# Moving the sample sequences' state updates from the mixing stage of a hybrid decoder layer into its second feed-forward block

## The chip, the cores and the metric

One core of a Trainium2 chip runs the whole program. The metric is the device time of one execution in microseconds, the median of several runs. The engines are TensorE (PE; PEld is its loading of weights), VectorE (DVE), ScalarE (ACT), GpSimd (POOL) and SyncE (SP, which here only issues DMAs).

## The reference

Two layers of a decoder work on 256 prompt tokens and on 8 sample sequences of 4 tokens each, 288 columns in all. The sample sequences bring carried states and return new ones:

```python
for l in range(DEPTH):
    x = layer_norm(ALPHA * x + 0.5 * swiglu(x, ffn1_w_in[l], ffn1_w_out[l]), ...)
    z = x @ mix_w_in[l]                       # split into RWKV-7, HGRN2 and chunk-gMLP heads
    ...
    mix = concat([o_rw, o_hg, o_cm]) @ mix_w_out[l]
    x = layer_norm(ALPHA * x + mix, ...)
    x = layer_norm(ALPHA * x + 0.5 * swiglu(x, ffn2_w_in[l], ffn2_w_out[l]), ...)

# RWKV-7, each token (state S is value by key, 4 heads of 64 x 64 for each sequence)
S = S * w_t + sa (kk_t a_t)^T + v_t k_t^T ;  o_t = S r_t
# HGRN2 (state is 128 x 128, 4 heads for each sequence)
S = exp(total) * S + sum_s k_s exp(total - cum_s) v_s^T
```

The outputs of the sample tokens need the old states and the four tokens' own rows. The new states are outputs of the program and are read by nothing else in it.

## The kernel before

Activations lie with features on the 128 rows and the 288 tokens as columns. Every dense product is made of 128x128 weight blocks; for precision, weights and operands are split into a high and a low part, and three products are summed (`block`). A block of weights of 512x256 is loaded by SP into `raw` (three buffers), rounded by ACT into `wh`, and its rest is made by DVE, in places by POOL, into `wl` (`prep`, three buffers each).

A layer has three stages: a feed-forward block (`ffn`), the mixing stage (`mix`) and a second feed-forward block. A feed-forward block runs over 11 steps j of 256 columns. Each has a gate and an up product of 48 matmuls each; DVE and ACT scale, shift and multiply them (`zfix`). Then the output product and a layer norm follow (`post`). `ffn` takes a table `mid` of functions that are called ahead of a step; in the second block of a layer and in layer 1's first, step 2 gets the `residual`, eight chunks of two DVE operations and one ACT operation.

The mixing stage interleaves chains, which are Python generators, with the dense products of the input projection as a background (`go`, `CHAINS`, `ORDER`): `prompt`, `pre` and `post` for RWKV-7, `scan` and `hmix` for HGRN2's prompt tokens, `sample` (`rw_sample`) and `hsam` (`hg_sample`) for the sample tokens, `cm` for the gMLP, and the `hou`/`posts` chains that write the operand tiles of the output product. Two chains make the new states:

- `rst` (`rw_states`, line 1255) starts when `sample` is done. `rw_sample` has already made, on POOL, the operands `ub`: the corrections `uv` spread over the 8 sequences. For each of two head pairs PE makes `pns` (a product with `ex`), DVE adds it to the state tile `st`, and POOL multiplies `st` by the decay read from `eP`. Then PE transposes `st` (`pno`), ACT copies it to `no`, and SP issues eight stores.
- `hst` (`hg_states`, line 1541) starts when `hsam` is done. For each of four heads the value rows are spread over the sequences into `hvb`, on ACT for heads 0 and 2 (8 scalings each) and on POOL for heads 1 and 3; POOL multiplies the loaded state `hs` by the decay in `hgP`; PE makes two products `hn`; DVE adds each to half of `hs`; SP issues one store of 512 KB.

The list scheduler of the framework orders each engine's instructions when the program is built: by the order in which they are traced, the lead that `PR` gives a part, and its model of when operands and tile buffers are ready. On the chip each engine then follows that fixed order and waits where an operand is late. Tiles of a tag share a number of buffers (`B`: 19 large `m4` tiles, 11 of `a2`).

The program prints `act`, `mul`, `add` and the like as one helper line each (L62, L65, L77 in the profile), so operations are told apart by their tiles.

Of the kernel before, what the change touches and what calls it, by code (L numbers as in the profile page):

```python
# [2 lines left out]

# [35 lines left out]
class Trunk:  # L39
# [80 lines left out]
    def consts(self):  # L120
# [34 lines left out]
        # causal masks over [s, t]: t > s and t >= s  # L155
# [5 lines left out]
        # block-merge masks: ml[b][t, s] and mt[b][s, t]  # L161
# [13 lines left out]
        # the same for blocks of 64 tokens, in rows of (block parity, token)  # L175
# [19 lines left out]
        # sample block masks over [(h,s), (h,t)], blocks of four tokens  # L195
# [9 lines left out]
        # the same with the rows of head h at the place of head (h + 2) % 4  # L205
# [3 lines left out]
        # row -> batch within a 32-token group, and row -> parity of its head  # L209
# [10 lines left out]
        # sums over a head's 64 rows into 32 equal rows, and their spreading back  # L220
# [11 lines left out]
        # a token's row in each group of 32; minus one at odd rows  # L232
# [3 lines left out]
        # two heads' inclusive sample blocks in either half of the rows  # L236
# [17 lines left out]
        # a token's row in each group of 32, for either pair of heads  # L254
# [3 lines left out]
        # the first four rows repeated for each batch  # L258
# [3 lines left out]
        # token -> batch, and a token's row in each group of 32  # L262
# [4 lines left out]
        # reset points of the running sums: token 0 of each chunk  # L267
# [70 lines left out]
    def prep(self, spec):  # L338
        """A block of weights, loaded and split into high and low parts."""
# [34 lines left out]
    def block(self, spec, x, res, first, last):  # L374
        """A block's share of a product."""
# [26 lines left out]
    def dense_by(self, w, n0s, x, groups):  # L402
        """Several products, each group of chunks through all of them before the next."""
# [7 lines left out]
    def fill(self, n=1):  # L411
        """Goes on with the products in the background by n steps."""
# [18 lines left out]
    def hilo(self, r, name, n=NT):  # L431
        """Rows of high and low parts in turn, of equal rows."""
# [5 lines left out]
    def newx(self, nt):  # L438
        """Operand tiles of a product's moving side: eight 128-row chunks, high and low parts."""
# [9 lines left out]
    def zfix(self, ps, st, nm):  # L449
        """A product's two column blocks, and their biases, with the norm's scale (and shift) applied."""  # L450
# [45 lines left out]
    def post(self, wout, x, nk, coef, ln, shift, groups=None):  # L496
        """Residual sum with a product, and its layer norm: the operand tiles of the next product hold
        (u - m) g in high and low parts, with m the mean of the first six chunks (shift) or of all."""
# [100 lines left out]
    def final(self, po, m6, coef, g, square, i):  # L599
        """The last norm, in rows of tokens, and the outputs; the last rows are the prompt's end and the samples."""  # L600
# [6 lines left out]
        def rows(j, c):  # L607
            """A chunk, times the norm's gain, in rows of tokens."""
# [40 lines left out]
        # the mean's rest as rows of high, low and high parts  # L649
# [34 lines left out]
    def final_load(self, l):  # L684
        """The last norm's shift in each row, and its gain in (negated) rows of high, high and low parts."""
# [10 lines left out]
    def residual_g(self, pend):  # L696
        """The norm's output itself, times ALPHA for the next residual sum."""
# [9 lines left out]
    def residual_x(self):  # L707
        """The same, and operand tiles of it."""
# [11 lines left out]
    def load_x(self, specs):  # L720
        """The operand tiles of the inputs; both loads in halves of the features, and the first weights between."""
# [66 lines left out]
    def rw_pre(self, l, q, zs):  # L788
# [3 lines left out]
        # lora products  # L792
# [3 lines left out]
        else:  # L796
            # tanh(x) = 2 sigmoid(2 x) - 1
# [19 lines left out]
        # running sums of the log decay (in units of -exp(-0.5)), centred in each chunk  # L817
# [17 lines left out]
        # keys  # L835
# [30 lines left out]
        # (sum r k r_k) v, and the norm's shift  # L866
# [13 lines left out]
    def gnorm(self, l, x, n):  # L880
        """Rows of tokens, less the means of n groups of 64, and one over each group's deviation."""
# [12 lines left out]
    def rw_gate(self, q, OT, p, G, BO, m, ts):  # L894
        """The norm's gain and shift, the bonus and the gate, into chunks 0 and 1 of the operand tiles m."""
# [33 lines left out]
    def rw_prompt(self, l, KR, bh, kh, V, eP, em):  # L929
        """Four chunks of 64 tokens; rows are (chunk parity, token), matrices [rows, chunk pair, head, token]."""  # L930
# [8 lines left out]
        # token-major values, first keys beside AT[1] in the order of its matrices, second keys  # L939
# [15 lines left out]
        def heads(j=None, i=None):  # L955
            """Chunk pair, parity, head pair, head, its rows, its columns and its matrix."""
# [7 lines left out]
        def pairs(name, f):  # L964
            """Products of both head parities, in turn in the array's two row halves."""
# [9 lines left out]
        for qi, src in ((0, bh), (2, kh)):  # L975
# [13 lines left out]
            if qi == 0:  # L989
                # the inverse over pairs of tokens, and its transpose  # L990
# [12 lines left out]
        # token-major values, keys and (negated) first operands  # L1003
# [15 lines left out]
        # inverses over twice as many tokens, from I - (the block between two halves) times the inverse  # L1019
# [25 lines left out]
        # corrections without the state, and their dependence on it  # L1045
# [11 lines left out]
        # from one chunk's state to the next, and to the outputs  # L1057
# [3 lines left out]
        # decay from a chunk's centre to its end, and on to the next chunk's centre  # L1061
# [36 lines left out]
        # token-major outputs  # L1098
# [31 lines left out]
    def rw_load(self, l):  # L1130
        nc, I = self.nc, self.I
        # carried states, rows (parity of the batch, value)
# [7 lines left out]
    def rw_sample(self, l, KR, bh, kh, V, eP):  # L1140
# [9 lines left out]
        # the carried states transposed to rows (head, key)  # L1150
# [8 lines left out]
        # keys and queries of each batch alone  # L1159
# [4 lines left out]
        # A matrices: rows (h, s), or (h + 2, s) for those that meet values  # L1164
# [19 lines left out]
        # [row, head pair, head, token]: rows A_rb and A_rk of each pair  # L1184
# [11 lines left out]
        # token-major values (rows swapped by two heads) and keys  # L1196
# [8 lines left out]
        # rows of each pair block-expanded by head  # L1205
# [18 lines left out]
        # solve for the corrections  # L1224
# [6 lines left out]
        # the queries' products  # L1231
# [16 lines left out]
        ub = [v512(self.a2(f"ub{l}{c}")) for c in range(2)]  # L1248
        for c in range(2):
            self.mul(ub[c].rearrange("p (b v) -> p b v", b=8), uv[:, c].unsqueeze(1).to_broadcast([128, 8, 64]),  # L1250
                     self.mb.unsqueeze(2).to_broadcast([128, 8, 64]), gp)
        yield
        self.rws = ST, exv, ub, eP

    def rw_states(self, l):
        """The sample states after their tokens."""
        nc, O = self.nc, self.O
        gp = nc.gpsimd
        SS = slice(T, NT)
        ST, exv, ub, eP = self.rws  # L1260
        no = self.m4([128, 2, 4, 2, 64], f"no{l}")
        for c in range(2):
            p = self.ps(f"pns{l}{c}")
            self.mm(p, exv[:, c].rearrange("p h n -> p (h n)"), ub[c])
# [276 lines left out]
    def hg_states(self, l):  # L1541
# [5 lines left out]
        for h in range(4):  # L1547
# [10 lines left out]
            if h in E["hs"]:  # L1558
                self.mul(s0, s0, tot.to_broadcast([128, 8, 128]), gp)
# [273 lines left out]
```

## Time and profile before

| | us |
|---|---|
| runs of the kernel | 1373.8, 1374.07, 1381.42 |
| median | 1374.07 |
| span of the profiled execution | 1379.8 |
| PE busy | 1308.3 (95%) |
| DVE busy | 1009.8 (73%) |
| ACT busy | 663.8 (48%) |
| POOL busy | 274.1 (20%) |

The span is the time from the first to the last instruction of the one execution that was profiled. The stages of layer 0 lie at about 10 to 240 us (first feed-forward block), 240 to 485 us (mixing, with its output product and norm) and 485 to 690 us (second feed-forward block); layer 1 repeats them up to 920, 1155 and 1375 us. In the rows below, an instruction row of a timeline has start, duration, engine, source line, operation, output and inputs, shapes and count; a bracket at its end is the idle time before it and what ended it. Neighbouring instructions of one kind are merged into one row with a count.

### The profile page before, as it was taken

The page shows a single profiled execution, that of the slowest core. Times are in us where ns is not written, and L with a number is a line of the kernel's source. Part 1 is how long each engine was busy: PE and PEld are TensorE (multiplying, and loading weights), DVE is VectorE, ACT ScalarE, POOL GpSimd, SP SyncE. Part 2 cuts the span into 40 slices and gives each one's busy share as a digit, 9 for nine tenths or more (in the row PEclk, how much of TensorE's full clock was granted, in tenths as well). Part 3 has the DMA queues.
Part 4 walks back from the last instruction along what each step waited for, and adds up shares of the span by engine and source line. Part 5 has one row for each costly group of instructions (what it writes and reads, how often), then busy time and mean ns, then how long its engine had stood idle before and what let it go on. Part 6 is the DMA issues. An engine that isn't in the chain of part 4 may idle for free.

```text
span 1379.8 us, 27635 instructions
## 1 busy us (share of the span) xinstructions
PE 1308.3 (95%) x11161; PEld 1255.1 (91%) x11162; DVE 1009.8 (73%) x1844; ACT 663.8 (48%) x1052; POOL 274.1 (20%) x381
## 2 busy tenths in 40 slices
PE   7999999898987999999999999998889889999998
PEld 6999999877876999999999999997778789999997
DVE  3555448977877998774698775599986889977643
ACT  4454435762345554443465443368333645544433
POOL 9200001435554100000100000033464421000002
PEclk9999999987997999999999999999999889999999
DMA  5655554531123655554455555554212544555551
GB/s 175 187 168 168 162 165 150 154 106 34 48 86 113 187 156 158 165 168 153 155 168 167 167 156 161 167 160 131 78 31 71 149 124 145 168 161 161 175 168 58
DMA packets 208158, 194.12 MB, mean 141 GB/s; under 512 B 15911, under 2 KB 206363, under 8 KB 208030
## 3 DMA queue, kind: packets, MB, share of 16 engines
q1 hardware_dynamic: 207326, 190.91, 44.9%
q0 software_dynamic: 608, 1.31, 0.4%
q8 instruction: 88, 1.44, 0.4%
q14 instruction: 40, 0.33, 0.1%
q10 hardware_dynamic: 96, 0.13, 0.1%
HBM read 185.10 MB, written 7.22 MB: 139 GB/s over the span
## 4 chain that ended last, share of the span: by engine, by line
PE 79%; DVE 14%; issue 3%; ACT 2%; POOL 1%; DMA 0%; POOLq 0%; SPq 0%; DVEq 0%; ACTq 0%
PE d L97 71%; DVE wl L65 2%; DVE hgO L77 1%; ACT wh L62 1%; DVE yrw L77 1%; DVE hgQ L77 1%; PE pA L97 1%; DVE hR L65 1%; DVE hAT L94 1%; PE hO L97 0%; PE hA L97 0%; DVE ax L65 0%; PE pD L97 0%; POOL hgP L65 0%; DVE hL L65 0%
## 5 line engine op out<-in xcount | busy, mean ns | idle before, releaser
L97 PE MATMUL d<-x,wh 128*128 128x290 f32 (+1 forms) x3968 | 824.0, 301 | 2.5 <-DVE x L77 2.5
L97 PEld LDWEIGHTS d<-x,wh 128*128 128x128 f32 x3968 | 653.3, 192 | 9.8 <-DVE x L77 4.3
L97 PE MATMUL d<-x,wl 128*128 128x290 f32 (+1 forms) x1984 | 602.5, 304 | 16.2 <-ACT x L62 12.4
L62 ACT ACTIVATE wh<-raw 128x1024 fp32r<-128x1024 f32 x344 | 357.2, 1039 | 456.1 <-PE d L97 312.1
L65 DVE TENSOR_TENSOR wl<-raw,wh 128x1024 fp32r<-128x1024 f32 x324 | 395.1, 1220 | 239.4 <-ACT wh L62 238.1
L97 PEld LDWEIGHTS d<-x,wl 128*128 128x128 f32 x1984 | 380.5, 192 | 21.5 <-ACT x L62 15.5
L97 PE MATMUL d<-h,wh 128*128 128x288 f32 x1408 | 282.0, 296 | 0.0
L97 PEld LDWEIGHTS d<-h,wh 128*128 128x128 f32 x1408 | 226.2, 188 | 0.2
L97 PE MATMUL d<-h,wl 128*128 128x288 f32 x704 | 207.8, 295 | 0.0
L65 POOL TENSOR_TENSOR lnv<-lnq,lnq 128x288 f32<-128x288 f32 x6 | 8.2, 1375 | 848.7 <-ACT lnq L62 848.7
L97 PEld LDWEIGHTS d<-h,wl 128*128 128x128 f32 x704 | 132.5, 188 | 0.2
L65 POOL TENSOR_TENSOR wl<-raw,wh 128x1024 fp32r<-128x1024 f32 x20 | 50.0, 2502 | 66.3 <-ACT wh L62 66.3
L62 ACT ACTIVATE h<-sg 128x288 fp32r<-128x288 f32 x88 | 38.1, 435 | 24.5 <-DVE sg L65 20.9
L62 ACT ACTIVATE sg<-yg,ccg 128x288 f32<-128x288 f32 x66 | 34.3, 528 | 29.9 <-DVE yg L77 29.9
L62 ACT ACT_TABLE_LOAD x37 | 47.5, 1283 | 1.4 <-PEq L1821 0.8
L65 DVE TENSOR_TENSOR h<-sg,h 128x288 fp32r<-128x288 f32 x88 | 39.6, 452 | 5.6 <-ACT h L62 5.6
L77 DVE SCALAR_TENSOR_TENSOR ax<-d,ax 128x288 f32<-128x288 f32 x48 | 21.4, 452 | 29.4 <-PE d L97 29.4
L77 DVE SCALAR_TENSOR_TENSOR yu<-nu,ccu,yu 128x288 f32<-128x288 f32 x66 | 33.9, 514 | 0.8
L77 DVE SCALAR_TENSOR_TENSOR yg<-nu,ccg,yg 128x288 f32<-128x288 f32 x66 | 33.8, 515 | 0.8
L62 ACT ACTIVATE lnq<-ax 128x288 f32<-128x288 f32 x48 | 20.9, 435 | 26.2 <-DVE ax L77 26.0
L77 DVE SCALAR_TENSOR_TENSOR sg<-yu,ccu,sg 128x288 f32<-128x288 f32 x66 | 33.3, 509 | 0.0
L65 DVE TENSOR_TENSOR yu<-d,rho 128x288 f32<-128x288 f32 x66 | 29.5, 448 | 0.0
(499 smaller groups left out, 1355.2 us busy)
## 6 DMA issues: line engine op xcount, KB each, us to landing
raw<-in_ffn_w_in SPq DMA_DIRECT2D x176, 512.0 KB
raw<-in_ffn_w_out SPq DMA_DIRECT2D x80, 512.0 KB
raw<-in_mix_w_in SPq DMA_DIRECT2D x56, 512.0 KB
raw<-in_mix_w_out SPq DMA_DIRECT2D x12, 512.0 KB
raw<-in_ffn_w_out SPq DMA_DIRECT2D x16, 256.0 KB
hs<-in_state_hgrn SPq DMA_DIRECT2D x8, 512.0 KB
out_hgrn_state_sample<-hs SPq DMA_DIRECT2D x8, 512.0 KB
raw<-in_mix_w_out SPq DMA_DIRECT2D x8, 256.0 KB
```

The costliest lines, as they stand in the source:

```text
L62: self.nc.scalar.activation(out, in_, func, **kw)
L65: (eng or self.nc.vector).tensor_tensor(out, a, b, op=op)
L77: self.nc.vector.scalar_tensor_tensor(out, a, s, b, op0=op0, op1=op1)
L94: self.nc.vector.copy_predicated(out, mask.bitcast(I16), data)
L97: self.nc.tensor.matmul(out, lhsT, rhs, start=start, stop=stop)
```

## The change

The chains `rst` and `hst` leave the mixing stage. Their steps, now one generator of 12 steps, are called in the second feed-forward block of the same layer: two steps each ahead of the column steps 1, 3, 4, 5, 6 and 7. So step 1 has the RWKV state sums, step 3 their transposes and stores, and steps 4 to 7 one HGRN2 head each. `ub` is made there too, on POOL. The decays are copied by ACT into small tiles (`dc`, `tot`) at the end of the sample chains, since `eP` and `hgP` do not live that long. In `hg_states` the variants go: all spreading is done on ACT, and instead of a multiplication on POOL and an addition on DVE, DVE does both in one scalar_tensor_tensor for each sequence and head.

```diff
 # rw_sample
-        ub = [v512(self.a2(f"ub{l}{c}")) for c in range(2)]
-        for c in range(2):
-            self.mul(ub[c]..., uv[:, c]..., self.mb..., gp)
-        yield
-        self.rws = ST, exv, ub, eP
+        dc = self.ep.tile([128, 2, 8], F32, tag="rdc", name=f"rdc{l}", bufs=1)
+        self.act(dc, eP[:, :, SS].rearrange("p c (b t) -> p c b t", t=4)[:, :, :, 3])
+        yield
+        self.rws = ST, exv, uv, dc
...
 # rw_states
         for c in range(2):
+            ub = self.a2(f"ub{l}{c}").rearrange("p c n -> p (c n)")[:, 0:512]
+            self.mul(ub.rearrange("p (b v) -> p b v", b=8), uv[:, c].unsqueeze(1).to_broadcast([128, 8, 64]),
+                     self.mb.unsqueeze(2).to_broadcast([128, 8, 64]), gp)
             p = self.ps(f"pns{l}{c}")
-            self.mm(p, exv[:, c].rearrange("p h n -> p (h n)"), ub[c])
+            self.mm(p, exv[:, c].rearrange("p h n -> p (h n)"), ub)
             stc = ST[:, c]
             self.add(stc, stc, p.rearrange("p (b v) -> p b v", b=8))
-            dc = eP[:, c, SS].rearrange("p (b t) -> p b t", t=4)[:, :, 3:4].to_broadcast([128, 8, 64])
-            self.mul(stc, stc, dc, gp)
+            self.mul(stc, stc, dc[:, c].unsqueeze(2).to_broadcast([128, 8, 64]), gp)
             yield
...
 # hg_sample
-        yield
-        self.hst = S0, k3
+        tot = self.ep.tile([128, 4, 8], F32, tag="htot", name=f"htot{l}", bufs=1)
+        self.act(tot, self.hsm(P).rearrange("p h (b t) -> p h b t", t=4)[:, :, :, 3])
+        yield
+        self.hst = S0, k3, tot
...
 # hg_states
-            if h in E["vb"]:
-                for b in range(8):
-                    self.act(vb[:, b], v, scale=self.mb[0:96, b:b + 1])
-            else:
-                self.mul(vb, v.unsqueeze(1).to_broadcast([96, 8, 128]),
-                         self.mb[0:96].unsqueeze(2).to_broadcast([96, 8, 128]), gp)
-            tot = self.hsm(P)[:, h].rearrange("p (b t) -> p b t", t=4)[:, :, 3:4]
-            if h in E["hs"]:
-                self.mul(s0, s0, tot.to_broadcast([128, 8, 128]), gp)
+            for b in range(8):
+                self.act(vb[:, b], v, scale=self.mb[0:96, b:b + 1])
             yield
             for i in range(2):
                 p = self.ps(f"hn{l}{h}{i}")
-                bs = slice(4 * i, 4 * i + 4)
-                self.mm(p, k3[0:96, 0, h], vb[:, bs].rearrange("p b v -> p (b v)"))
-                if h in E["hs"]:
-                    self.add(s0[:, bs], s0[:, bs], p.rearrange("p (b v) -> p b v", b=4))
-                else:
-                    for b in range(4):
-                        bb = 4 * i + b
-                        self.stt(s0[:, bb], s0[:, bb], tot[:, bb], p[:, 128 * b:128 * b + 128], ALU.mult, ALU.add)
+                self.mm(p, k3[0:96, 0, h], vb[:, 4 * i:4 * i + 4].rearrange("p b v -> p (b v)"))
+                for b in range(4):
+                    bb = 4 * i + b
+                    self.stt(s0[:, bb], s0[:, bb], tot[:, h, bb:bb + 1], p[:, 128 * b:128 * b + 128], ALU.mult, ALU.add)
...
 # run
-            r = self.ffn(l, "ffn2_w_in", "ffn2_w_out", x, st, lambda: q[l]["ln"][2], {2: self.residual}, SHIFT[2])
+            states = chain(self.rw_states(l), self.hg_states(l))
+            mid = {j: lambda: (next(states), next(states)) for j in STATES} | {2: self.residual}
+            r = self.ffn(l, "ffn2_w_in", "ffn2_w_out", x, st, lambda: q[l]["ln"][2], mid, SHIFT[2])
...
 # mix
-            "hst": (lambda: self.hg_states(l), "hsam"),
-            "rst": (lambda: self.rw_states(l), "sample"),
...
-CHAINS = [('prompt', 1), ('pre', 3), ('rst', 1), ('hsam', 1), ('posts', 1), ('hst', 1), ('hmix', 1), ('sample', 1),
+CHAINS = [('prompt', 1), ('pre', 3), ('hsam', 1), ('posts', 1), ('hmix', 1), ('sample', 1),
...
+STATES = (1, 3, 4, 5, 6, 7)
```

In `PR` the entry `'hst.6': 100` goes, in `E` the entries `'vb'` and `'hs'`. Everything else in the diff is comments.

## Rows read from the trace of the kernel before

**Rows 1.** The page: busy time, share of the span and instructions of each engine.

```profile
PE 1308.3 (95%) x11161; PEld 1255.1 (91%) x11162; DVE 1009.8 (73%) x1844; ACT 663.8 (48%) x1052; POOL 274.1 (20%) x381
```

**Rows 2.** Waits of PE, 240 to 485 us: us in total, times, longest.

```profile
PE d L97 <- ACT x L62: 6.2, 1, 6.2
...
PE cO L97 <- DVE cM L65: 5.7, 1, 5.7
...
PE pb L97 <- DVE rn L77: 2.6, 1, 2.6
...
PE d L97 <- DVE ax L77: 0.6, 1, 0.6
```

**Rows 3.** Timeline, 425 to 450 us: start, us, engine, line, operation, count, idle before.

```profile
428.06 1.20 DVE L77 SCALAR_TENSOR_TENSOR hgO<-yo,cco,qs 128x256 f32<-128x256 f32 x4
...
431.69 6.23 DVE L77 SCALAR_TENSOR_TENSOR hgO<-yo,cco,qs 128x256 f32<-128x256 f32 x4
...
432.04 7.99 POOL L65 TENSOR_TENSOR hs<-hs,hgP 128x1024 f32<-128x1024 f32 x4 [8.89 <-PE hp L97]
...
433.64 0.26 ACT L62 ACTIVATE hsqs<-hp 128x128 f32<-128x128 f32 x1
...
437.84 2.46 DVE L65 TENSOR_TENSOR OT<-OT,G 128x256 f32<-128x256 f32 x2
...
438.28 0.42 ACT L62 ACTIVATE x<-OT 128x256 fp32r<-128x256 f32 x1 [4.38 <-DVE OT L65]
...
438.75 0.61 PE L97 MATMUL d<-x,wl 128*128 128x288 f32 x1 [6.20 <-ACT x L62]
...
442.34 0.40 DVE L65 TENSOR_TENSOR x<-OT,x 128x256 fp32r<-128x256 f32 x1
```

**Rows 4.** Timeline, 1098 to 1116 us: the same place in layer 1.

```profile
1108.13 0.61 PE L97 MATMUL d<-x,wl 128*128 128x288 f32 x1 [6.18 <-ACT x L62]
```

**Rows 5.** Windows after both waits: PE, PEld, DVE, ACT, POOL busy; granted clock, DMA.

```profile
438.70:447.30 8.60, 7.62 (x33) 7.28 (x34) 5.53 (x10) 3.00 (x10) 5.25 (x4) 0.51 0.00 0
...
1108.10:1116.80 8.70, 7.75 (x35) 7.40 (x36) 5.62 (x11) 3.09 (x10) 5.23 (x3) 0.53 0.00 1
```

**Rows 6.** Windows of steps 1, 2, 3 and 7, second feed-forward block of layer 0.

```profile
498.80:511.50 12.70, 12.70 (x97) 12.70 (x96) 12.37 (x27) 7.66 (x12) 0.00 (x0) 1.00 0.54 166
...
511.50:524.30 12.80, 12.75 (x95) 12.54 (x94) 12.72 (x29) 8.02 (x12) 0.00 (x0) 1.00 0.53 165
...
524.30:537.10 12.80, 12.80 (x98) 12.80 (x97) 10.82 (x23) 6.14 (x9) 0.00 (x0) 1.00 0.50 161
...
575.40:588.20 12.80, 12.80 (x98) 12.80 (x97) 9.96 (x21) 5.84 (x8) 0.00 (x0) 1.00 0.54 164
```

**Rows 7.** Tiles: count, ns least/median/most, first and last start, forms.

```profile
L65 POOL TENSOR_TENSOR ub<-uv,mb x4: 1041/1132/1255, 334.7 to 1002.0; 128x512 f32<-128x512 f32 x4
...
L65 DVE TENSOR_TENSOR st<-st,pns x4: 671/676/686, 342.3 to 1018.3; 128x512 f32<-128x512 f32 x4
...
L65 POOL TENSOR_TENSOR st<-st,eP x4: 1057/1062/1069, 345.1 to 1019.1; 128x512 f32<-128x512 f32 x4
...
L62 ACT ACTIVATE hvb<-hk,mb x32: 385/387/390, 447.4 to 1123.5; 96x128 fp32r<-96x128 f32 x32
...
L77 DVE SCALAR_TENSOR_TENSOR hSP<-hSP,hgP,hS x8: 339/342/347, 451.3 to 1121.1; 128x128 f32<-128x128 f32 x8
```

**Rows 8.** Timelines of SP's queue and of ACT: store issues, a weight load, its use.

```profile
355.74 7.32 SPq L1278 DMA_DIRECT2D out_rwkv_state_sample<-no  x8
...
537.39 0.37 SPq L347 DMA_DIRECT2D raw<-in_ffn_w_in  x1
...
544.69 1.06 ACT L62 ACTIVATE wh<-raw 128x1024 fp32r<-128x1024 f32 x1 [2.14 <-PE d L97]
```

**Rows 9.** Windows of 4 us after the wait for rn in layers 0 and 1.

```profile
302.00:306.00 4.00, 4.00 (x21) 2.28 (x20) 3.33 (x7) 1.07 (x2) 0.00 (x0) 0.50 0.00 0
...
976.00:980.00 4.00, 2.45 (x20) 1.68 (x20) 4.00 (x11) 0.85 (x2) 0.78 (x1) 1.00 0.00 0
```

More of the change, by code (lines that the diff above doesn't have):

```diff
@@ L2 @@
 from contextlib import ExitStack, contextmanager
+from itertools import chain
 import concourse.bass as bass
@@ L1247, in rw_sample @@
         self.act(self.rwos, pq)
-        ub = [v512(self.a2(f"ub{l}{c}")) for c in range(2)]
-        for c in range(2):
-            self.mul(ub[c].rearrange("p (b v) -> p b v", b=8), uv[:, c].unsqueeze(1).to_broadcast([128, 8, 64]),
-                     self.mb.unsqueeze(2).to_broadcast([128, 8, 64]), gp)
+        dc = self.ep.tile([128, 2, 8], F32, tag="rdc", name=f"rdc{l}", bufs=1)
+        self.act(dc, eP[:, :, SS].rearrange("p c (b t) -> p c b t", t=4)[:, :, :, 3])
         yield
-        self.rws = ST, exv, ub, eP
+        self.rws = ST, exv, uv, dc
     def rw_states(self, l):
@@ L1258, in rw_states @@
         gp = nc.gpsimd
-        SS = slice(T, NT)
-        ST, exv, ub, eP = self.rws
+        ST, exv, uv, dc = self.rws
         no = self.m4([128, 2, 4, 2, 64], f"no{l}")
         for c in range(2):
+            ub = self.a2(f"ub{l}{c}").rearrange("p c n -> p (c n)")[:, 0:512]
+            self.mul(ub.rearrange("p (b v) -> p b v", b=8), uv[:, c].unsqueeze(1).to_broadcast([128, 8, 64]),
+                     self.mb.unsqueeze(2).to_broadcast([128, 8, 64]), gp)
             p = self.ps(f"pns{l}{c}")
-            self.mm(p, exv[:, c].rearrange("p h n -> p (h n)"), ub[c])
+            self.mm(p, exv[:, c].rearrange("p h n -> p (h n)"), ub)
             stc = ST[:, c]
             self.add(stc, stc, p.rearrange("p (b v) -> p b v", b=8))
-            dc = eP[:, c, SS].rearrange("p (b t) -> p b t", t=4)[:, :, 3:4].to_broadcast([128, 8, 64])
-            self.mul(stc, stc, dc, gp)
+            self.mul(stc, stc, dc[:, c].unsqueeze(2).to_broadcast([128, 8, 64]), gp)
             yield
@@ L1537, in hg_sample @@
         self.hos = os
+        tot = self.ep.tile([128, 4, 8], F32, tag="htot", name=f"htot{l}", bufs=1)
+        self.act(tot, self.hsm(P).rearrange("p h (b t) -> p h b t", t=4)[:, :, :, 3])
         yield
-        self.hst = S0, k3
+        self.hst = S0, k3, tot
     def hg_states(self, l):
         nc, O = self.nc, self.O
-        gp = nc.gpsimd
-        P = self.hg("P")
-        S0, k3 = self.hst
+        S0, k3, tot = self.hst
         for h in range(4):
@@ L1782 @@
 PR = {'prep': 250, 'posts': 450, 'hou0': -50, 'scan': 400, 'hsam': -150, 'post': -400, 'res': 50, 'scan.4': 20,
-      'cm.1': 200, 'q1.0': -7, 'hmix': 20, 'hst.6': 100, 'sample.0': -20, 'hmix.7': -20, 'posts@1': -400,
+      'cm.1': 200, 'q1.0': -7, 'hmix': 20, 'sample.0': -20, 'hmix.7': -20, 'posts@1': -400,
       'sample.2': 50, 'houts@0': 200, 'prompt.19': -7, 'houts': 50, 'scan@0': 400, 'houts.0': -50, 'prompt.22': 200,
       'o1': 7}
-E = {'gn': 'v', 'gm': 'v', 'LN': 1, 'th': 't', 'xl': 'p', 'R1': 'p', 'mo': 'r', 'om': '', 'vb': (0, 2), 'hs': (0, 1,
-     2, 3), 'Ab': 'p', 'RV': 'v', 'LL': 'v', 'S': 'p', 'P': 'p', 'KS': 'v'}
+E = {'gn': 'v', 'gm': 'v', 'LN': 1, 'th': 't', 'xl': 'p', 'R1': 'p', 'mo': 'r', 'om': '', 'Ab': 'p', 'RV': 'v', 'LL': 'v', 'S': 'p', 'P': 'p', 'KS': 'v'}
 GROUPS = {'s': ((0, 1), (6, 7), (2, 3, 4, 5)), 't': ((6, 7), (0, 1), (2, 3, 4, 5)), 'r': ((0, 1, 6, 7), (2, 3, 4,
```

## The prediction

> **What bounds the kernel now.** I read the busy shares first: PE is busy 95% of the span, no other engine above 73% [rows 1]. So time can only be won where PE waits or runs at a low clock. In the two feed-forward blocks of a layer PE does neither (12.75 to 12.80 us busy in each 12.8 us step, clock 1.00) [rows 6]. What is to be won lies in the mixing stage, some 240 to 485 us in layer 0 and its copy in layer 1. The list of PE's waits for that stretch has one largest item: the output product waits 6.2 us, once, for ACT's operand tile x; after it come 5.7, 2.6 and many below 2 us [rows 2]. Layer 1 waits 6.18 us at the same place [rows 4].
>
> The timeline around that wait tells what is late. Four scalar_tensor_tensor on DVE (hgO) start at 431.69 and take 6.23 us; the same four shapes took 1.20 us at 428.06. In between, at 432.04, POOL starts four products hs*tot of 128x1024, 7.99 us in one row. The first OT products, also on DVE, follow and end only when POOL is through (2.46 us for two); then ACT splits OT at 438.28, and PE starts at 438.75 [rows 3]. All the slow DVE instructions read two operands from SBUF, as POOL does. The windows show a second cost: in the 8.6 us after the wait the granted clock is 0.51 (layer 1: 0.53 over 8.7 us), PE's lower level of 1.2 GHz, and PE is still idle for 8.60 - 7.62 = 0.98 us of it [rows 5].
>
> **The change, part by part.**
>
> *POOL's four hs*tot and two vb products leave the mixing stage (per layer).* Without them hgO takes its 1.20 us and ends at 431.69 + 1.20 = 432.89. The next OT product has the operands of the x split, 0.40 us [rows 3], so 433.3. ACT is then still busy: it ends hsqs at 433.64 + 0.26 = 433.90. PE started 438.75 - 438.28 = 0.47 us after the split did, so now at 434.37: a wait of some 1.8 us is left, and 438.75 - 434.37 = 4.38 us are won.
>
> *The clock.* Does it still fall after 1.8 us? The nearest rows are two equal waits of 2.6 us for rn: after the one of layer 0 the clock is 0.50, after that of layer 1 it is 1.00 [rows 2, 9]. [...] If the clock holds, the 7.62 busy us at 0.51 shrink to 7.62 x 0.51 = 3.9, and the 0.98 us of idleness, which is DVE's lateness handed on, mostly goes: 8.6 - 3.9 - 0.2 = 4.5 us won. If it falls all the same, only the 0.98 us is won. I take 4.5 and keep 1.0 as the other end.
>
> *The additions hs + hn on DVE leave the output product.* PE's wait for ax behind them, 0.6 us [rows 2], goes.
>
> Per layer: 4.38 + 4.5 + 0.6 = 9.5 us with the clock held, 4.38 + 0.98 + 0.6 = 6.0 without. Two layers: 19 or 12.
>
> *PE's moved products* (pns, pno, hn) keep their shapes and number, so what the mixing stage saves the feed-forward block pays: zero. This would be a loss if they had filled PE's waits; they stand on the chain or beside dense products, so I see none. A gain in the middle of the mixing stage from POOL's freed time (two ub of 1.13 and two st of 1.06 us, 4.4 us per layer [rows 7]) lies between 0 and 4.4; the dense products there hide most of it, so I take 0. The two added copies (tot, dc) are small ACT work like hsqs, at most 2 x 0.26 us, at a place where ACT waits anyway.
>
> *What the second feed-forward block gets.* Its cover is DVE's and ACT's free time per step; PE has none. Steps 4 to 7 each get one head: 8 ACT scalings of 0.387 us = 3.1 us [rows 7] beside 5.84 busy us of 12.8 [rows 6], which fits; and 8 DVE scalar_tensor_tensor of 128x128 reading PSUM, a form that hSP shows at 0.342 us [rows 7]: 2.74 us beside 9.96 of 12.80 [rows 6], which leaves 0.1 us. It just fits. Step 1 is worse: two additions st of 0.68 us = 1.35 on DVE, and 4.4 us of POOL work that can hold DVE as it held hgO. DVE has 0.33, 0.08 and 1.98 us free in steps 1 to 3, since the residual's work is there already [rows 6]. So DVE is late by up to 1.35 + 4.4 - 2.4 = 3.3 us and has no room to catch up before step 8. What PE bears of it is shown by the residual: in its step DVE is busy 12.72 of 12.80 us and PE still does its 95 products in 12.75 us. So the price lies between 0 and 3.3 us per layer; I take 1.4, nearer to the end that the residual shows. The Trainium skill speaks against this part: "SBUF — State Buffer", section "Who interferes with whom", says that a DVE instruction with two SBUF inputs and a GpSimd instruction that reads SBUF exclude each other for a whole instruction, while one with a single SBUF input is not held. By it the zfix products that read PSUM pass, the zfix additions and the low parts of the weights are held, and the new scalar_tensor_tensor never are; the block's price would be the upper 3.3 us.
>
> *Queues.* Twelve stores per layer move along SP's queue into the block: eight of the RWKV state (7.32 us of SP time for the eight, waits included) and four of HGRN2's. Behind a store that waits for DVE or ACT stand the weight loads. A load is issued at 537.39 and, with three raw buffers, first read by the fourth scaling, at 544.69 [rows 8]: 7.3 us less the transfer. A delay of a few us is hidden; I price it at zero. POOL has nothing else in this block, so nothing stands behind ub there [rows 6].
>
> *Sum:* 2 x (9.5 - 1.4) = 16 us. The profiled execution has a span of 1379.8 us, 5.7 above the median of the runs (1374.07) and within them (1373.8 to 1381.42); it would come to 1363.8. The same 16 us from the median give **1358 us**.
>
> **The rivals.**
>
> *Half is given back (1366).* The clock falls after 1.8 us too, or DVE's lateness reaches PE: 12 - 2 x 1.4 = 9, or 19 - 2 x 3.3 = 12 with part of the first. For it: the two unequal outcomes at 2.6 us, and 0.1 us of room in steps 4 to 7. Against: PE's undisturbed steps under the residual. About 8 us faster, 1366.
>
> *Nothing is won (1374).* PE would then wait as long for the next late operand in the same place: ACT's table load ends just before hsqs, and hon, hO and the second hot follow one another. Against it: these follow the same late DVE row, and the 0.98 us is all that PE waited for them.
>
> *Slower: PE waits behind the moved products (1391).* PE takes its products in order. In step 1 pns needs ub from POOL, and pno needs st from POOL, which needs DVE, whose order is full; hn needs eight ACT scalings. If such a product stands in PE's order ahead of its operand, the dense products behind it wait. The wait at cO is of this kind: 5.7 us [rows 2], and a fallen clock after it costs up to half of the following 8 us [rows 5], some 9 us together. Two such waits per layer cost 36 us, net 36 - 19 = 17 us slower, 1391. It decides from one such wait per layer on, where the gain is gone. Against it: ub's inputs lie ready long before the block.
>
> *More is won (1346).* POOL's 4.4 us per layer in the middle of the mixing stage do shorten the chain there, and the block pays nothing: 19 + 8.8 = 28 us.
>
> **Chances.** Forecast 0.56 (its own range 1350 to 1364), half given back 0.18, nothing 0.09, slower 0.09, more 0.08. About 1% (13.7 us) is what a measurement of this kernel tells from no change; the line is 1360.3. Four fifths of the forecast's chance, the case of more, and a little of the half lie below it: 0.45 + 0.08 + 0.02 = 0.55 faster. Within 1%: 0.11 + 0.16 + 0.09 = 0.36. Slower: 0.09. The range from 1347 to 1374 leaves out the slower case (0.09), half of "nothing" and half of "more": 0.175.
>
> **What would show it.** Right: PE's first output product waits under 2 us in both layers, hgO takes about 1.2 us there, and the following window's clock is above 0.9. If the wait is short but the clock is still near 0.5, the clock's step fails. In the second feed-forward block each step should stay near 12.8 us plus the moved products; waits of PE for wl, y or x there would show that DVE's room was too small, and waits of pns, pno or hn for POOL, DVE or ACT that the order was wrong. SP rows of the stores that are followed by late weight loads would put the loss on the queue. The prediction is wrong altogether if hgO stays at 6 us with POOL idle: then POOL was not what held DVE.

## The result and the profile after: 1395 us, slower

The changed kernel takes 1395.28 us (median; 1389.42 to 1400.03) beside 1374.26 us for the kernel before on the same chip: a ratio of 1.0133, 95% interval 1.0092 to 1.0173. The forecast was 1358 us. The profiled execution has a span of 1398.3 us beside 1379.8.

The page's totals, against [rows 1]: PE is as busy a share as before, in a longer span; POOL has 12 instructions and 9 us less, DVE and ACT have 88 instructions more between them.

```profile
PE 1318.6 (94%) x11162; PEld 1257.7 (90%) x11162; DVE 1005.7 (72%) x1892; ACT 681.2 (49%) x1092; POOL 265.0 (19%) x369
```

The stages, cut at the start of each norm's pair of `lnva` products on PE (the last stage runs to the end of the span), in us. The columns are the mixing stage and the second feed-forward block of layer 0 and of layer 1; the first feed-forward blocks differ from before's by 1 us or less. The kernels below the first two are the experiments. Each ratio is to runs of the kernel before on the same chip. The stages are those of the one execution that was profiled, which need not be a median one: the spans of before, after, hp_without_hs and only_hgrn_moved are 1379.8, 1398.3, 1384.5 and 1355.2 us.

| kernel | median | ratio to before, 95% | mix 0 | FFN2 0 | mix 1 | FFN2 1 |
|---|---|---|---|---|---|---|
| before | 1374.3 | | 251.6 | 212.0 | 243.9 | 224.8 |
| after | 1395.3 | 1.0133 (1.0092–1.0173) | 257.5 | 216.7 | 246.7 | 230.0 |
| before_no_steps | 1394.8 | 1.0133 (1.0097–1.0170) | 252.9 | 211.7 | 256.7 | 224.3 |
| idle_steps_back | 1364.4 | 0.9894 (0.9842–0.9947) | 238.9 | 215.9 | 230.7 | 230.3 |
| posts_steps_three | 1362.7 | 0.9883 (0.9840–0.9925) | 237.4 | 215.9 | 228.4 | 230.5 |
| only_hst_idle_steps | 1399.0 | 1.0127 (1.0065–1.0189) | 256.9 | 216.7 | 249.2 | 228.1 |
| idle_steps_no_states | 1355.4 | 0.9847 (0.9812–0.9883) | 238.9 | 211.5 | 230.7 | 224.6 |
| no_root | 1389.5 | 1.0099 (1.0065–1.0132) | 254.1 | 216.6 | 240.2 | 230.7 |
| sample_steps_two | 1381.3 | 1.0038 (1.0010–1.0066) | 248.2 | 216.0 | 240.9 | 230.6 |
| hp_without_hs | 1378.4 | 1.0020 (0.9985–1.0054) | 248.0 | 215.9 | 242.5 | 230.6 |
| rwkv_sample_steps_two | 1363.6 | 0.9898 (0.9865–0.9930) | 235.0 | 216.0 | 234.7 | 229.0 |
| before_no_pool | 1376.4 | 1.0006 (0.9982–1.0031) | 242.3 | 212.4 | 246.1 | 224.9 |
| only_hgrn_moved | 1361.6 | 0.9886 (0.9840–0.9932) | 232.5 | 213.5 | 233.9 | 227.5 |
| only_rwkv_moved | 1384.8 | 1.0061 (1.0034–1.0089) | 250.8 | 213.6 | 242.7 | 227.2 |

So after's loss lies in two places: the second feed-forward blocks got longer by 4.7 and 5.2 us, which the move has to pay, and the mixing stages, out of which work was taken, got longer too, by 5.9 and 2.8 us (the two profiles against each other).

The DVE timeline at the place of [rows 3]: the four hgO in question take 1.20 us, where they took 6.23.

```profile
430.76 1.20 DVE L78 SCALAR_TENSOR_TENSOR hgO<-yo,cco,qs 128x256 f32<-128x256 f32 x4
```

PE's waits in layer 0's mixing stage (us in total, times, longest), against [rows 2]: the 6.2 us for x are 1.8 and the 5.7 us at cO are gone, and the largest is a new one, 8.4 us for hos; hT's and hTs's are new as well.

```profile
PE hot L102 <- ACT hos L63: 8.4, 1, 8.4
...
PE hT L102 <- ACT hvs L63: 3.3, 1, 3.3
...
PE d L98 <- ACT x L63: 1.8, 1, 1.8
PE hTs L102 <- DVE cM L66: 1.7, 1, 1.7
```

PE's timeline there: the instructions that waited, and cO. hTs is the first transpose of HGRN2's sample chain, hT are other transposes of HGRN2, cO is the gMLP's product, and hot are the transposes of hon (the prompt tokens' result) and hos (the sample tokens') that open the last chains of HGRN2.

```profile
415.84 1.09 PE L98 MATMUL cO<-cwt,cvn 128*64 128x128 f32 x16
...
419.46 0.33 PE L102 MATMUL hTs<-ident,hgV 128*128 128x128 f32 x1 [1.70 <-DVE cM L66]
...
423.55 1.12 PE L102 MATMUL hT<-ident,hgV 128*128 128x128 f32 x4 [3.27 <-ACT hvs L63]
...
429.19 0.40 PE L98 MATMUL d<-x,wl 128*128 128x288 f32 x1 [1.82 <-ACT x L63]
...
456.50 0.48 PE L102 MATMUL hot<-ident,hos 128*128 128x128 f32 x1 [8.38 <-ACT hos L63]
```

In the kernel before, hTs and the first half of cO came at 406.6 and 408.0, and the transpose of hos came last of the hot, without a wait:

```profile
406.60 0.27 PE L101 MATMUL hTs<-ident,hgV 128*128 128x128 f32 x1
...
408.00 0.66 PE L97 MATMUL cO<-cwt,cvn 128*64 128x128 f32 x8 [0.18 <-POOL cvn L65]
...
450.27 0.27 PE L101 MATMUL hot<-ident,hos 128*128 128x128 f32 x1
```

ACT's timeline shows what hos waited for. ACT alternates between the sigmoids of the background's last product (qs<-yo,cco) and the roots of HGRN2's norm (hrm, hrm0s), and loads its function table four times, 1.28 us each.

```profile
448.16 0.28 ACT L63 ACTIVATE hsqs<-hp 128x128 f32<-128x128 f32 x1 [9.13 <-PE hp L98]
448.45 1.28 ACT L63 ACT_TABLE_LOAD   x1
449.75 0.54 ACT L63 ACTIVATE qs<-yo,cco 128x288 f32<-128x288 f32 x1
450.30 1.28 ACT L63 ACT_TABLE_LOAD   x1
451.60 0.30 ACT L63 ACTIVATE hrm<-hrm,eps 128x4 f32<-128x4 f32 x1
...
452.33 1.28 ACT L63 ACT_TABLE_LOAD   x1
453.63 0.53 ACT L63 ACTIVATE qs<-yo,cco 128x288 f32<-128x288 f32 x1
454.18 1.28 ACT L63 ACT_TABLE_LOAD   x1
455.48 0.29 ACT L63 ACTIVATE hrm0s<-hrm0s,eps 128x1 f32<-128x1 f32 x1
...
456.10 0.35 ACT L63 ACTIVATE hos<-hp,hrm0s 128x128 f32<-128x128 f32 x1
```

The same stands in layer 1 (a wait of 8.38 us at 1133.44). Behind the transpose of hos in PE's order stand those of hon, which DVE had finished at 438.9 (the first half) and 452.8; PE could not take them. The dense products behind those had not all been ready: the first started at 457.78, just after DVE had made an x (457.28, 0.45 us), which stands in DVE's order behind ho, a product that needs hot. In the kernel before, the sigmoids of that product ran at 426.5 and 431.0.

### The profile page after: what moved, and what is told of

Same layout as the page of the kernel before. It is cut to its first block, busy times and chain, and to the rows that moved or that the text cites. A ratio compares the mean times of both kernels' runs of the same rounds, so it can differ in the third digit from the quotient of the medians.

```text
span 1398.3 us, 27677 instructions
## 1 busy us (share of the span) xinstructions
PE 1318.6 (94%) x11162; PEld 1257.7 (90%) x11162; DVE 1005.7 (72%) x1892; ACT 681.2 (49%) x1092; POOL 265.0 (19%) x369
## 5 line engine op out<-in xcount | busy, mean ns | idle before, releaser
L66 POOL TENSOR_TENSOR lnv<-lnq,lnq 128x288 f32<-128x288 f32 x6 | 8.2, 1374 | 837.7 <-ACT lnq L63 837.7
```

Of the source, the lines that this page charges most:

```text
L66: (eng or self.nc.vector).tensor_tensor(out, a, b, op=op)
```

## The experiments

The theory after reading this: the change takes more out of the mixing stage than work. `go` lets the background products go on by one step after each step of a chain (`fill`). With `rst` and `hst` twelve steps left, and twelve background steps with them. The order that the scheduler then builds is another one, and worse. The rival: the order is the same in effect, and moved work itself costs the 21 us.

**Idle steps in the place of `rst`.** Four steps that do nothing, with their background steps; the states stay in the feed-forward block.

```diff
+            "rst": (lambda: iter([None] * 4), "sample"),
...
-CHAINS = [('prompt', 1), ('pre', 3), ('hsam', 1), ...
+CHAINS = [('prompt', 1), ('pre', 3), ('rst', 1), ('hsam', 1), ...
```

> The changed kernel, but with a chain of four empty steps where the RWKV state chain stood in the mixing stage, so that the four background steps of dense products that followed its steps are traced where they were before. Theory A (the loss is the order: without these background steps the products o1 and o0 and the loads of hs come later in the plan, ScalarE alternates between two tables, PE waits 8.4 us for hos per layer): the hos wait and the added table loads (41 to 37) go, hs is loaded before the last output weights, the 6.2 us wait of before does not come back, and the time is near the forecast, 1350 to 1365 us. Theory B (the loss is the states held in large buffers through the mixing stage, or the moved work itself): nothing of that changes, the time stays at 1390 to 1400 us.

Measured: 1364.4 us, 31 us below after and some 1% below before. PE's waiting instructions in its timeline: hTs stands before cO again, the transpose of hos comes last of the hot and waits for nothing, and at the output product's place PE waits 1.14 us, at the first hot, for ACT's x.

```profile
405.37 0.27 PE L102 MATMUL hTs<-ident,hgV 128*128 128x128 f32 x1
...
414.02 1.12 PE L98 MATMUL cO<-cwt,cvn 128*64 128x128 f32 x8 [5.72 <-DVE cM L66]
...
433.74 0.30 PE L102 MATMUL hot<-ident,hon 128*128 128x128 f32 x1 [1.14 <-ACT x L63]
...
440.29 0.27 PE L102 MATMUL hot<-ident,hos 128*128 128x128 f32 x1
```

By the stage table the mixing stages are 18.6 and 16.0 us shorter than after's, 34.6 together; the difference of the two spans is the same 34.6. All of it is order: four empty steps are the only difference. 21.5 us of it are PE's idle time (66.4 against 44.8 us in both mixing stages), and 13.1 us are longer busy time for the same number of matmuls, which was not taken apart. The sums of the two stages, after and then idle steps:

```profile
sum 504.23, PE 437.87 PEld 386.54 DVE 387.57 ACT 250.49 POOL 194.96; mean PE 218.94 PEld 193.27 DVE 193.79 ACT 125.25 POOL 97.48
```

```profile
sum 469.57, PE 424.75 PEld 382.10 DVE 384.65 ACT 244.50 POOL 186.74; mean PE 212.38 PEld 191.05 DVE 192.33 ACT 122.25 POOL 93.37
```

**Before, without the background steps.** The states stay where they were; only the numbers behind two chains change.

```diff
-CHAINS = [('prompt', 1), ('pre', 3), ('rst', 1), ('hsam', 1), ('posts', 1), ('hst', 1), ...
+CHAINS = [('prompt', 1), ('pre', 3), ('rst', 0), ('hsam', 1), ('posts', 1), ('hst', 0), ...
```

> The kernel before, states still made in the mixing stage, but no background step after the steps of the two state chains (1 to 0 for both in the list of chains). Theory A: the tail takes the order of the changed kernel, hs is loaded after the last output weights, a wait for hos appears, and the time rises to 1390 to 1410 us though nothing is moved. Theory B: same buffers and same work as before, so 1370 to 1380 us.

Measured: 1394.8 us, the loss of the change without the change. PE's waits in layer 0 have after's new rows:

```profile
PE hot L101 <- ACT hos L62: 7.7, 1, 7.7
PE d L97 <- ACT x L62: 6.1, 2, 4.1
PE hT L101 <- ACT hvs L62: 3.0, 1, 3.0
```

Which steps, and does the chain matter? Two runs. First, idle steps for `hst` alone:

```diff
+            "hst": (lambda: iter([None] * 8), "hsam"),
...
-CHAINS = [... ('posts', 1), ('hmix', 1), ...
+CHAINS = [... ('posts', 1), ('hst', 1), ('hmix', 1), ...
```

> The changed kernel with an idle chain for hst alone: eight steps that do nothing, each followed by one background step, as hst had them before; rst stays out. hst starts only when hsam is done, late in the mixing stage, where little of the background is left. Theory A, only the four steps of rst set the order: hot<-hos stays ahead of the dense products, PE waits some 8 us for hos in each layer, 1389 to 1400 us. Theory B, the number of lost steps counts and eight given back are more than enough: 1362 to 1372 us.

Measured: 1399.0 us. Eight steps late in the stage give nothing back. Second, no idle chain, but three background steps instead of one behind each step of `posts`, which starts where `rst` did:

```diff
-CHAINS = [... ('posts', 1), ...
+CHAINS = [... ('posts', 3), ...
```

> The changed kernel with one number different: each step of the chain posts, which like rst starts when sample is done, is followed by three background steps instead of one; there are no idle steps. The loads of hs then stand ahead of four loads of mix_w_out as in the kernel with idle steps, hot<-hos stands last of the three hot products, and there are 37 table loads instead of 41. Theory A, what was lost with rst is only the progress of the background products at that place, whoever gives it: 1360 to 1368 us, as with the idle steps. Theory B, the place of rst itself counts: 1375 to 1395 us.

Measured: 1362.7 us. What counts is how far the background is when `sample` is done, not who drives it.

**What in the bad order costs.** Four runs of the changed kernel, with a number, a function or an operand changed. The root of the HGRN2 norm without its table:

```diff
-        self.act(r, r, AF.Sqrt, bias=self.eps[:, 2:3], scale=1.0 / 128)
+        self.act(r, r, AF.Square, scale=1.0 / 128)
```

> The changed kernel, in which the root of the HGRN2 norm (hrm, hrm0s) is made by ACT as a square, without the added eps; the values that come out of the HGRN2 norm are then others than the reference's. PE's order is the changed kernel's own, hot<-hos stands first as there; what goes is ACT's table loads between the sigmoids and the roots, four of 1.28 us in the last 10 us ahead of hos. Theory A, the table loads are the larger part of the wait for hos: it falls from 8.4 to about 3.3 us in layer 0, and the time by twice that and some clock, to 1379 to 1387 us. Theory B, hos is late for its operands and not for the tables: the wait stays at 7 to 8 us, the time at 1391 to 1397.

Measured: 1389.5 us. PE's order in the mixing stages stayed, matmul for matmul. The wait for hos fell from 8.4 to 4.5 us, but the time by 5.8 us only, less than expected: the tables are half of that wait and about a fifth of the 31 us.

```profile
452.21 0.47 PE L102 MATMUL hot<-ident,hos 128*128 128x128 f32 x1 [4.46 <-ACT hos L63]
```

The Trainium skill, "ScalarE: Activation LUTs", section "Table sets: the hidden batching unit", asks that all calls of one set be made before those of the next. The trace agrees: the sigmoids and roots that alternate paid four loads of 1.28 us, those of the order with idle steps one between them.

Next, two background steps behind each step of `hsam`, which brings the transpose of hos to the last place of the hot and the sigmoids ahead of the roots:

```diff
-CHAINS = [... ('hsam', 1), ...
+CHAINS = [... ('hsam', 2), ...
```

> The changed kernel with one number different: each step of the chain hsam is followed by two background steps instead of one. Nothing is moved or left out. In the order as built this brings the product hot<-hos to the last place of the three hot products and puts ACT's two sigmoids ahead of the roots, but the loads of hs still stand as late in SP's queue as in the changed kernel (behind eight loads of mix_w_out). Theory A, the loss is PE's standing behind hos (8.4 us in a layer, with the clock that falls after it): the wait for hos is gone and the time comes to about 1362 to 1370 us, as with the idle steps. Theory B, a good part of the loss is the late load of hs, with hp in between the dense products: the time stays at 1378 to 1395 us.

Measured: 1381.3 us, within the range of the second theory. 14 of the 31 us are gone with the wait for hos; 17 are still there. PE's timeline shows where: hTs and hT still stand behind cO, and everything of HGRN2 after them.

```profile
417.50 0.33 PE L102 MATMUL hTs<-ident,hgV 128*128 128x128 f32 x1 [1.73 <-DVE cM L66]
...
422.54 1.11 PE L102 MATMUL hT<-ident,hgV 128*128 128x128 f32 x4 [4.12 <-ACT hvs L63]
...
448.69 0.73 PE L102 MATMUL hot<-ident,hon 128*128 128x128 f32 x4 [3.14 <-DVE hon L66]
```

It could be that place, or the loads of hs, which SP issued at 424.0 here and at 414.1 and 418.8 with idle steps, with the products hp that need them. Two runs were made to tell these apart: two background steps for `sample` instead, and the kernel just shown with hp reading a constant.

```diff
-CHAINS = [... ('sample', 1), ...
+CHAINS = [... ('sample', 2), ...
```

> The changed kernel with one number different: each step of the chain sample is followed by two background steps instead of one. In the order as built, hot<-hos is the last of the three hot products, and HGRN2's first transposes hTs and hT stand ahead of the gMLP's product cO, as in the kernel with idle steps (with two steps of hsam's own, the kernel before this one, they stand behind cO). The loads of hs stand one place later than with idle steps, and hp alternates one by one with dense products, as in the changed kernel. Theory A, the second half of the loss (1381 us with hsam's two steps against 1364) is HGRN2's transposes standing behind cO, so that its chain to hot ends the mixing stage: 1362 to 1370 us. Theory B, it is hp's place between the dense products behind the late hs: 1377 to 1385 us.

```diff
-                self.mm(p[32 * h:32 * h + 32], qm[:, h, b], S0[h][:, b], b == 0, False)
+                self.mm(p[32 * h:32 * h + 32], qm[:, h, b], self.ident, b == 0, False)
```

> The kernel with two background steps for each step of hsam (1381 us), in which the products hp read a constant tile in the place of the loaded states hs, so the outputs of HGRN2's sample tokens lack their states; hs is still loaded for the new states. The order built then has half of hp at once behind the transposes; hTs and hT stay behind cO. Theory A, the place of the transposes behind cO makes the second half of the loss: the time stays, 1376 to 1384 us. Theory B, it is the late hs with hp: 1362 to 1372 us.

Measured: 1363.6 us with hTs ahead of cO, and 1378.4 us without the need for hs. The first run doesn't tell the two apart as hoped: its order has the loads of hs early as well (issued at 398.6), and hp is mostly in one piece. The second does: with nothing to wait for, 26 of the 64 hp ran at 427.3 already, and 1378.4 us stand beside 1381.3. So the late hs is not the second half of the loss. That the place of HGRN2's chain behind cO is, the first run does not show either. PE is idle as long in its two mixing stages as in those of the kernel with two steps of `hsam` (55.6 and 55.1 us; 44.8 with idle steps). The 19 us between their stages are PE's busy time for the same number of matmuls, at a granted clock of 0.95 and 0.95 against 0.90 and 0.93. Its order is another in over half of its places from early in the stage on, and part of its gain lies far ahead of cO: at pb in layer 0 PE waited 1.45 us and the clock was 1.00 behind it, where the other had 2.73 us and 0.50. So what makes the second half stays open. The sums of the two stages, two steps of `hsam` and then of `sample`:

```profile
sum 489.06, PE 433.94 PEld 386.20 DVE 387.47 ACT 239.88 POOL 194.73; mean PE 216.97 PEld 193.10 DVE 193.73 ACT 119.94 POOL 97.36
```

```profile
sum 469.65, PE 414.01 PEld 373.97 DVE 381.60 ACT 242.98 POOL 186.67; mean PE 207.00 PEld 186.99 DVE 190.80 ACT 121.49 POOL 93.33
```

PE's timeline in that run:

```profile
396.44 0.27 PE L102 MATMUL hTs<-ident,hgV 128*128 128x128 f32 x1
...
396.66 0.60 PE L102 MATMUL hT<-ident,hgV 128*128 128x128 f32 x4
397.19 0.66 PE L98 MATMUL cO<-cwt,cvn 128*64 128x128 f32 x8
...
427.92 1.08 PE L102 MATMUL hot<-ident,hon 128*128 128x128 f32 x4 [3.80 <-DVE hon L66]
```

**What the moved work costs, and which part earns the gain.** The version with idle steps, with the states neither made nor stored:

```diff
-STATES = (1, 3, 4, 5, 6, 7)
+STATES = ()
```

> As the first of this job, but the new states of the sample sequences are neither made nor stored in the second feed-forward block (rw_states and hg_states are left out, so these two outputs are not written). The difference to the first run is the price of the moved work in that block. If it is only PE's own products (second feed-forward blocks of the changed kernel are 4.7 and about 5 us longer, without any wait of PE), 9 to 11 us less than the first run; if DVE's lateness or the stores cost more, 14 us or more.

Measured: 1355.4 us, 9.0 less; by stages 4.4 and 5.7 us of the second feed-forward blocks and nothing of the mixing stages. Then each half of the move alone, with the order kept by `rst` (real or idle):

```diff
 # only_hgrn_moved: rst real, hst moved
-            states = chain(self.rw_states(l), self.hg_states(l))
+            states = self.hg_states(l)
...
+            "rst": (lambda: self.rw_states(l), "sample"),
...
-STATES = (1, 3, 4, 5, 6, 7)
+STATES = (4, 5, 6, 7)
 # only_rwkv_moved: rst idle and moved, hst as before, with POOL's products
-            states = chain(self.rw_states(l), self.hg_states(l))
+            states = self.rw_states(l)
...
+            "hst": (lambda: self.hg_states(l), "hsam"),
+            "rst": (lambda: iter([None] * 4), "sample"),
...
-STATES = (1, 3, 4, 5, 6, 7)
+STATES = (1, 3)
```

> Only HGRN2's states are moved: hst leaves the mixing stage and has its steps ahead of the column steps 4 to 7 of the second feed-forward block, rst stays in the mixing stage as a chain with its background steps (ub is made in its steps now). If POOL's products for hst were what held hgO, and the order goes bad through the lost steps of rst alone, then the output product's wait falls from 6.2 to below 3 us and nothing waits for hos: 1360 to 1367 us, a little below the version with idle steps, since the second feed-forward block gets four products and 32 scalings fewer on its steps 1 and 3 and ub doesn't stand on POOL beside hgO. If the lost steps of hst count as well: 1380 to 1395 us.

> Only RWKV's states are moved, ahead of the steps 1 and 3 of the second feed-forward block; rst stays as four idle steps with their background steps, hst stays in the mixing stage as before, with POOL's products. If the gain of the version with idle steps is POOL's hst products alone, the 6.2 us wait of the output product stays and the time is that of before or a few us above it, since the second feed-forward block gets pns and pno: 1372 to 1379 us. If RWKV's part earns it (POOL's ub and st in the middle of the mixing stage), 1364 to 1370 us.

Measured: 1361.6 and 1384.8 us. HGRN2's half earns all of it; RWKV's alone loses, more than expected. Its timeline (DVE and POOL) shows that POOL's products still hold hgO, and that `ub`, no longer wanted early, runs at the end of the same stretch. How much that costs is not shown: in the profiles the mixing stages are 0.8 and 1.2 us shorter than before's, the second feed-forward blocks 1.6 and 2.4 us longer, and the spans differ by 2.5 us where the ratio of the runs gives 8.4.

```profile
430.16 4.62 DVE L78 SCALAR_TENSOR_TENSOR hgO<-yo,cco,qs 128x256 f32<-128x256 f32 x4
...
430.54 8.74 POOL L66 TENSOR_TENSOR hs<-hs,hgP 128x1024 f32<-128x1024 f32 x4 [9.36 <-PE hp L98]
...
443.14 2.40 POOL L66 TENSOR_TENSOR ub<-uv,mb 128x512 f32<-128x512 f32 x2
```

**POOL out of `hst` without a move.** In the kernel before, DVE and ACT do POOL's part in the mixing stage:

```diff
-'vb': (0, 2), 'hs': (0, 1, 2, 3)
+'vb': (0, 1, 2, 3), 'hs': ()
```

> The kernel before with the HGRN2 states made in the mixing stage as the changed kernel makes them: all spreading on ScalarE, product and addition on DVE in one operation, nothing on POOL. If POOL holding DVE is the cause of the 6.2 us wait, four hgO take 1.2 us instead of 6.2, the wait falls to about 2 us in both layers, and the time falls by about 10 us to 1360 to 1368 us (the clock gain of 4.5 us per layer included, less some 3 us per layer for the longer DVE work beside the output product). If the wait has another cause it stays, and the time is 1372 to 1380 us.

Measured: 1376.4 us, no difference. The wait for x fell from 6.2 to 1.7 us, and PE waits 5.69 us for ax instead, behind DVE's 32 operations for hs (eight additions before):

```profile
446.10 3.96 DVE L77 SCALAR_TENSOR_TENSOR hs<-hs,hgP,hn 128x128 f32<-128x128 f32 x15
449.98 1.18 DVE L77 SCALAR_TENSOR_TENSOR ax<-d,ax 128x288 f32<-128x288 f32 x3
...
450.48 0.61 PE L97 MATMUL d<-x,wl 128*128 128x288 f32 x1 [5.69 <-DVE ax L77]
```

So here freeing POOL was worth something only together with taking the work out of the stage.

## Why the prediction was wrong

**The step that failed** is the one ahead of all the terms. The sum takes the timeline of before, leaves out POOL's products, shortens what stood behind them and lets every other row stand. That needs the other rows to keep their order. Here the order comes out of the program that traces them, and the prediction read `rst` and `hst` as work alone and not as twelve steps, each followed by a background step. Nothing in the sum or in the range is priced for a new order of the rows that stay. Four steps decided 31 us, about twice the gain forecast.

**The terms of the sum**, with the order kept (idle_steps_back), did come out, in total: 16.1 us by spans where 16 were forecast, 14.6 us by the ratio (1 - 0.9894, of 1374). But two of them were sized wrongly and made up for each other, which is luck: the mixing stages saved 25.9 us where 19 were forecast, and the second feed-forward blocks paid 9.4 where 2.8 were.

- *POOL's products hold DVE, without them the wait falls from 6.2 to 1.8 us:* right. After shows hgO at 1.20 us and waits of 1.82 and 2.42 us; before_no_pool shows the same fall with nothing moved. The Trainium skill's rule on the shared port ("SBUF — State Buffer", "Who interferes with whom") agrees once more: in idle_steps_back `ub` came early on POOL, at 432.83, and two hgO beside it took 1.59 us instead of 0.63.
- *The clock holds after a wait of 1.8 us:* no row of before shows the clock after such a wait at this place, so the 4.5 us were a choice between two ends. The windows of 8.6 us after the two waits for x, and after the wait for hos (PE, PEld, DVE, ACT, POOL busy; clock), against [rows 5], show it held in layer 0 of after only; 2.42 us in layer 1 are followed by 0.70. With idle steps, after a wait of 1.14 us, the windows 430 to 440 and 440 to 450 us both show 1.00. The 8.4 us for hos cost clock as well.

```profile
429.20:437.80 8.60, 7.66 (x62) 6.92 (x62) 2.96 (x9) 4.20 (x8) 0.00 (x0) 1.00 0.84 227
456.50:465.10 8.60, 8.44 (x44) 7.86 (x44) 6.91 (x15) 4.26 (x12) 0.00 (x0) 0.71 0.10 30
1104.90:1113.50 8.60, 8.60 (x51) 7.94 (x52) 4.30 (x9) 2.97 (x6) 2.26 (x2) 0.70 0.80 212
```

- *The second feed-forward block pays 1.4 us for DVE's lack of room:* wrong in kind and size. PE waits for nothing there. The windows of the whole block of layer 0, before and after, show PE full in both; the block is 4.7 us longer by PE's own products, 20 matmuls more (four pns, 1.88 us; eight pno, 1.03; eight hn of 0.4 us, or 0.63 for two in a row).

```profile
485.13:697.13 212.00, 211.95 (x1574) 210.99 (x1572) 159.09 (x295) 99.33 (x142) 5.40 (x5) 1.00 0.52 162
```

```profile
491.52:708.20 216.68, 216.68 (x1594) 214.67 (x1593) 169.76 (x329) 110.14 (x176) 8.53 (x7) 1.00 0.56 171
```

  DVE's 0.342 us for each operation was too much as well: five in a row took 1.37 us, each starting before the one ahead had ended. POOL did hold DVE in the block (sg took 1.30 us at 504.50, beside POOL's st, and 0.51 at 502.68), but PE waited for none of it: the upper price of 3.3 us, which the prediction tied to the rule of the Trainium skill, did not appear.
- *The moved products cost nothing, as the mixing stage saves what the block pays:* with the order kept it is near the truth. The mixing stages saved 12.7 and 13.2 us, 3.2 and 3.7 more than the 9.5 forecast without these products; the blocks paid 3.9 and 5.5. In after the mixing stage saved nothing, and the price of the block stood alone.
- *The middle of the mixing stage, taken as 0:* only_rwkv_moved saved 0.8 and 1.2 us of the mixing stages, and paid 1.6 and 2.4 in the blocks. The end chosen was right: that is less than the moved PE products alone take in the blocks.
- *The list of PE's waits* leaves out one of 4.6 us for sh, ahead of the changed place. It is 4.6 us in after as well and changes nothing.
- *SP's queue, zero:* right. The eight stores stood at 533.75 (5.26 us) and no load behind them made PE wait.

**The rivals.** The slower case (1391) came near the time for another reason. It had the mechanism in general, PE standing in order behind a product whose operand is late, and put it on the moved products in the wrong stage. The product was one that was not moved, the transpose of hos into hot, in the stage that the work had left.

## What to carry to other kernels

Where a program traces its work through interleaved generators and a scheduler builds the order, a chain is also a clock for what runs beside it: taking it out needs its ticks put back, here with one number. So ahead of a prediction, ask what each removed step drove, and don't take the largest wait in sight for the bound: here a new order cost 31 us, and the largest new wait was 8.4 us in each layer. When a move comes out slower in the very stage that got lighter, give the order back with empty steps first; that told work from order in one run.

## What was not expected of the hardware

The granted clock after one and the same wait differs from execution to execution. At pb in layer 0's mixing stage all the profiles but one show a wait of 2.6 to 2.7 us for rn, behind the same matmuls in the same order. In ten of these thirteen the clock is at its lower level after it and stays there for over 20 us; in three (before_no_steps, before_no_pool, only_hgrn_moved) it is 1.00. The four pb products take 2.29 us after it in the one case and 1.24 in the other. The next window of 20 us (columns as above), from after and from only_hgrn_moved:

```profile
306.00:326.00 20.00, 20.00 (x177) 16.11 (x174) 9.39 (x33) 3.70 (x9) 7.32 (x9) 0.52 0.26 79
```

```profile
306.00:326.00 20.00, 15.89 (x316) 13.29 (x315) 18.22 (x42) 5.99 (x14) 12.11 (x12) 1.00 0.31 97
```

The first did 177 matmuls in 20 us and was busy throughout, the second 316 in 15.9 us. Most of the 6.4 us by which only_hgrn_moved's first mixing stage is shorter than that of idle_steps_back lie in the 40 us behind pb: pb comes at the same time in both stages, and the first poS 5.8 us earlier (107.0 and 112.8 us after the stage's start). This is likely also most of the spread of single runs: of idle_steps_back's four, three took 1364.1 to 1365.4 us at a granted clock of 0.97, and one 1356.2 at 0.98. No run tried it apart. So a stage of one profile is compared with care where its clock differs. The two rows of [rows 9], the nearest that the forecast had for the clock, were two outcomes of one kind of wait, and tell nothing of a wait of 1.8 us.
